# Latent attention with undivided probabilities: each tile's outputs multiplied once by the heads' inverse sums, which are spread over the partitions through memory

## The chip, the core and the metric

The kernel runs on one core of a Trainium2 chip, as one program in one launch. The metric is the device time of that launch in microseconds (us). Before the change three runs took 1687.1, 1684.37 and 1682.98 us; their median, 1684.37 us, is the time before.

A core has a matrix engine (TensorE, in the profile PE, with its weight loads as PEld), a vector engine (VectorE, DVE), a scalar engine (ScalarE, ACT), a general engine (GpSimd, POOL) and a synchronizing engine (SP). Each runs its own instructions in order and waits for the others through semaphores. SBUF is the working memory of 128 partitions, PSUM the banks that PE writes its results to. DMAs move data between SBUF and the chip's memory; they are issued from the queues of SP, ACT and POOL.

## What is computed

Two layers of a diffusion backbone over 512 latent tokens and a prefix of 256 context tokens, 1024 wide, all in float32. Layer 0 mixes tokens by two groups of heads side by side: gated linear attention, and softmax attention with 8 query heads and 2 key and value heads of 64. Their outputs are joined and go through one output projection, then a SwiGLU block. Layer 1 is a gated recurrence and another SwiGLU block. The change is in the softmax attention of layer 0 alone:

```python
def _softmax_attend(q, k, v):
    s = jnp.einsum('bhgqd,bhkd->bhgqk', q, k, preferred_element_type=jnp.float32) * (ATT_HEAD_DIM ** -0.5)
    p = jax.nn.softmax(s, axis=-1).astype(v.dtype)
    return jnp.einsum('bhgqk,bhkd->bhgqd', p, v)
...
    o_blocks = lax.map(lambda qb: _softmax_attend(qb, k_all, va), q_blocks)
...
    o_lat = jnp.concatenate([a_lat, b_lat], axis=-1)
```

Latent queries see all 768 keys, context queries the 256 context keys. `a_lat` is the gated linear attention's half, `b_lat` the softmax attention's; their concatenation is what the output projection multiplies.

## The kernel before

Tokens lie in six tiles of 128: four latent (0 to 3) and two context (4 and 5). `even_mixer` writes layer 0's order out by hand: each piece of work is a generator under a short name ("x" is `att.context`, "y" is `att.latent`, "t" the transposes of the gated linear attention's outputs, "r1" a readout, "M" a group of modulation columns), and `run` steps them in a written sequence. With `pinned` set, PE keeps exactly that program order. DVE, ACT and POOL are ordered by a scheduler that knows the dependences; what it made of them is shown with the change.

`latent` is a pipeline over 32 heads, eight for each latent tile, one pass of its loop (L296) for a head. In pass i:

- `scores` (L178) computes the scores of head i into a two-bank PSUM tile `S` (two buffers). The keys are stored times -1/8, so the scores are negative and L193 on DVE takes a minimum to find the row's maximum. L195 on ACT exponentiates 128x768 scores into `prob` and sums each row into `asm`. L196 on DVE takes the reciprocal of that sum, L198 on DVE multiplies `prob` by it, in place.
- `turned` (L200) transposes the `prob` of head j = i - 3 on PE, six blocks of 128x128: four into a PSUM tile of two alternating ones, two into a single bank `sc`, and copies both pieces to `probT` (L210): 128x512 by ACT, and 128x256 by DVE for every fourth head (j % 4 == 3), by ACT for the other three.
- `values` (L212) multiplies, a pass after every second head was transposed, the `probT` of two heads by the values: 24 matrix instructions into one quarter of the bank `attO` (`self.po[t]`), head 2n in partitions 0 to 63 and head 2n + 1 in 64 to 127. When the fourth pair of a tile is in, `done` (L231) hands the bank to `put` (L732), which casts it on ACT (L734) and subtracts the cast from it on DVE (L735). The two results are a high and a low part that the output projection reads, since PE's fast float32 format keeps fewer bits.

There are two `sc` banks. Tile t's `attO` is bank t % 2, and the narrow transposes of the heads use the other one; after `done`, `other` (L148) gives them the bank just finished, until the next tile starts on its own. So the first narrow transposes after a tile's end write the bank that `put` reads, and have to wait until both its instructions are through. In the loop this is pass 12, 20 and 28: `done` is called in pass 8t + 11.

Behind the last pass come the output projection's matrix instructions (`oproj`; L1558). Its eight units of weights are loaded by SP (L768), cast on ACT (L769) and subtracted on DVE (L770). The buffers `raw` for the loads number three, so the last unit's load waits for an earlier unit's L770. The first pair of tiles it takes are the context tiles, over units 0 to 3 and then over units 4 to 7.

The 32-partition `gcT`, `gt` and `gd` of `gate_rows` (L638) do elsewhere what the change does here: eight or sixteen columns are transposed on PE, copied by DVE (L650) and stored to memory by ACT's queue (L652); L659 reads a row of it back to all partitions.

Of the kernel before, what the change touches and what calls it, by code (L numbers as in the profile page):

```python
# [8 lines left out]
F32 = mybir.dt.float32  # L9
# [4 lines left out]
ALU = mybir.AluOpType  # L14
# [3 lines left out]
P = 128  # L18
# [6 lines left out]
LT = SEQ // P  # L25
# [8 lines left out]
class Split:  # L34


    def __init__(self, pool):
        self.pool, self.tiles = pool, None
# [95 lines left out]
class Attention:  # L134
# [8 lines left out]

    def __init__(self, net, natq, natk, cat):
        self.net, self.nc, self.natq, self.natk, self.cat = net, net.nc, natq, natk, cat
        self.q, self.k, self.po, self.ended = {}, {}, {}, []

    def other(self):  # L148

# [25 lines left out]
            nc.vector.tensor_tensor(q[half[1 - n], 4 * n : 4 * n + 4, :], pv[half[n]], H.bitcast(F32), op=ALU.subtract)  # L175
        self.q[t] = q

    def scores(self, t, heads, p):  # L178

        nc, net = self.nc, self.net  # L180
        s = net.mm_tile("S")
        nk = p.shape[-1]
        w = 1024 // len(heads)
        for x, hd in enumerate(heads):
            at = w * x
            for ks in self.k[int(t >= LT)]:
                m = ks[0].shape[-1]
                for i, k in enumerate(ks):
                    net.mm(s[:, at : at + m], self.q[t][:, hd, :], k[:, hd // 4, :], start=(i == 0), stop=(i == 1))
                at += m  # L190
        sv = s.rearrange("p (x k) -> p x k", k=w)[:, :, :nk]
        mx, sm, r = (net.sm.tile([P, len(heads)], F32, tag=tag, name=tag) for tag in (("amx", "asm", "ars") if len(heads) == 1 else ("ms4", "ss4", "rs4")))
        nc.vector.tensor_reduce(mx, sv, axis=AX.X, op=ALU.min)  # L193
        for x in range(len(heads)):
            nc.scalar.activation(p[:, x, :], sv[:, x, :], AF.Exp, bias=mx[:, x : x + 1], scale=-1.0, accum_out=sm[:, x : x + 1])  # L195
        nc.vector.reciprocal(r, sm)  # L196
        for x in range(len(heads)):
            nc.vector.tensor_scalar(p[:, x, :], p[:, x, :], r[:, x : x + 1], None, op0=ALU.mult)  # L198

# [28 lines left out]
                    tile_position=(0, 64 * a),  # L228
                )

    def done(self, t):  # L231
        self.ended.append(t)
        self.net.put(self.cat, slice(4, 8), slice(t * P, (t + 1) * P), self.po[t].rearrange("p (j i) -> p j i", j=4))

    def context(self):
        wp = self.net.wp
# [23 lines left out]
        yield  # L260
        queries(LT + 1, "wL")
        scores(0)
        yield
        scores(1)
        yield
        turned(0)
        yield
        scores(2)
        values(0)
        yield  # L270
# [14 lines left out]
    def latent(self, ap):  # L285
        kl = [ap.tile([P, 2, SEQ], F32R, name=f"k{x}") for x in "HL"]
        self.k[0] = [kl] + self.k[1]
        q = lambda t: ap.tile([P, 8, P], F32R, tag="qs", bufs=2, name=f"qs{t}")
        self.keys(0, LT, kl)
        yield  # L290
        self.queries(0, q(0))
        yield

        ahead = 3
        ps, pTs, due = {}, {}, []
        for i in range(8 * LT + ahead + 2):  # L296
            t, hd = divmod(i, 8)
            if t < LT:
                ps[i] = ap.tile([P, NT], F32, tag="prob", bufs=4, name="prob")
                self.scores(t, (hd,), ps[i][:, None, :])  # L300
            j = i - ahead
            if 0 <= j < 8 * LT:
                pTs[j] = ap.tile([P, NTT, P], F32, tag="probT", bufs=4, name="probT")
                self.turned(ps.pop(j), pTs[j], (1,) if j % 4 == 3 else (), self.other())
            if due:
                t0, n, xs = due.pop()
                self.values(t0, n, xs)
                if n == 3:
                    self.done(t0)
            if 0 <= j < 8 * LT and j % 2:  # L310
                due.append((j // 8, j // 2 % 4, [pTs.pop(x) for x in (j - 1, j)]))
            if t + 1 < LT and hd == 4:
                self.queries(t + 1, q(t + 1))
            yield


class Net:
# [420 lines left out]
    def post_norm(self, y, x, gv, cuts=1, done=None):  # L738

        nc = self.nc  # L740
        cs = [slice(D // cuts * i, D // cuts * (i + 1)) for i in range(cuts)]
        tmp = self.wp.tile([P, WU], F32, tag="mraw", bufs=2, name="pn")
        ss = self.sm.tile([P, 4 if cuts > 1 else 1], F32, tag="ss4" if cuts > 1 else "ss", name="sq")[:, :cuts]
        for i, c in enumerate(cs):
            self.sumsq(y[:, c], ss=ss[:, i : i + 1])
            nc.vector.tensor_tensor(tmp[:, c], y[:, c], gv[:, c], op=ALU.mult)
        yield
        if cuts > 1:
            s = self.sm.tile([P, 1], F32, tag="ss", name="ss")
            nc.vector.tensor_reduce(s, ss, axis=AX.X, op=ALU.add)  # L750
            ss = s
        rs = self.rstd(ss, D)
        yield
        for c in cs:
            nc.vector.scalar_tensor_tensor(x[:, c], tmp[:, c], rs, x[:, c], op0=ALU.mult, op1=ALU.add)
            if done is not None:
                done(c)
        yield
# [1444 lines left out]
```

## Time and profile before

| What | Value |
|---|---|
| median of three runs | 1684.37 us (1682.98 to 1687.1) |
| the profiled execution | 1683.48 us, its span 1681.5 us |
| TensorE clock granted over the span | 0.999 |
| PE busy, whole span | 1644.6 us (98%) |
| DVE busy, whole span | 1309.8 us (78%) |
| ACT busy, whole span | 917.5 us (55%) |
| POOL busy, whole span | 121.4 us (7%) |
| the latent attention's 32 passes | about 255.6 to 346.5 us |

The span runs from the first instruction's start to the last one's end; the execution's own time is 1.98 us longer. All times of a timeline count from the span's start. In a timeline row stand start, length, engine, line, operation, what it writes and reads, the count of merged instructions, and in brackets the idle time of the engine before it with what ended it. A group's row ends in its busy time and the mean of one in ns, then the idle time before it.

### The profile page before, as it was taken

What the parts mean: (1) busy time and instruction counts of PE and PEld (TensorE: products, weight loads), DVE (VectorE), ACT (ScalarE), POOL (GpSimd) and SP (SyncE); (2) the same over time, 40 slices, a digit from 0 to 9 for tenths busy, and PEclk for the clock granted to TensorE, in tenths of its full rate; (3) what the DMA queues carried; (4) which work ended last, traced back from release to release, by engine and by line L of the source; (5) the groups of instructions that cost most, each with busy time, mean ns of one, the idle gap of its engine ahead of it and who ended that gap; (6) DMA issues with size and microseconds to landing.
All of it is one profiled execution on the core that took longest, in us unless ns stands there. A gap on an engine that the chain in (4) does not pass through costs nothing.

```text
span 1681.5 us, 32537 instructions
## 1 busy us (share of the span) xinstructions
PE 1644.6 (98%) x13407; PEld 1481.0 (88%) x13407; DVE 1309.8 (78%) x2105; ACT 917.5 (55%) x1560; POOL 121.4 (7%) x129
## 2 busy tenths in 40 slices
PE   6999998999999999999999999999999999999998
PEld 5899997888999999998888888888888899999876
DVE  4889768876898988877668548788775599987887
ACT  4745567836543443445447436666664565555654
POOL 1004110001000000003102000000000100000220
PEclk9999999999999999999999999999999999999999
DMA  9651002164243444348725542121124334333793
GB/s 330 192 155 41 2 27 101 51 207 152 84 147 101 144 143 148 117 150 167 142 73 203 190 129 59 51 64 39 52 64 150 125 111 117 113 101 101 183 206 138
DMA packets 184736, 204.79 MB, mean 122 GB/s; under 512 B 7142, under 2 KB 141836, under 8 KB 184588
## 3 DMA queue, kind: packets, MB, share of 16 engines
q1 hardware_dynamic: 173632, 181.82, 34.3%
q0 software_dynamic: 9024, 17.30, 5.9%
q10 hardware_dynamic: 1932, 3.59, 0.7%
q8 instruction: 105, 1.72, 0.4%
q14 instruction: 43, 0.35, 0.1%
HBM read 193.23 MB, written 9.46 MB: 121 GB/s over the span
## 4 chain that ended last, share of the span: by engine, by line
PE 85%; DVE 7%; ACT 3%; DMA 3%; issue 1%; POOL 0%; ACTq 0%; DVEq 0%; POOLq 0%
PE nat L355 13%; PE a L355 12%; PE ff L355 8%; PE E L355 8%; PE x L355 7%; PE oproj L355 6%; PE o L355 4%; PE D L355 4%; PE b L355 4%; PE fq L355 3%; PE gqk L355 2%; PE pearly L355 2%; PE S L355 2%; PE poh L355 1%; PE attO L355 1%
## 5 line engine op out<-in xcount | busy, mean ns | idle before, releaser
L355 PE MATMUL nat<-wH,x 128*128 128x256 f32 (+2 forms) x968 | 225.5, 321 | 3.0 <-ACT x L734 2.6
L355 PEld LDWEIGHTS nat<-wH,x 128*128 128x128 f32 x968 | 162.2, 190 | 19.2 <-ACT x L734 3.7
L824 ACT CAST wH<-raw 128x1024 fp32r<-128x1024 f32 x120 | 125.0, 1050 | 95.5 <-DVE raw L849 31.4
L825 DVE TENSOR_TENSOR wL<-raw,wH 128x1024 fp32r<-128x1024 f32 x120 | 145.6, 1220 | 21.3 <-ACT wH L824 20.9
L355 PE MATMUL nat<-wL,x 128*128 128x256 f32 (+2 forms) x484 | 153.4, 317 | 0.3 <-DVE wL L770 0.3
L770 DVE TENSOR_TENSOR wL<-raw,wH 128x1024 fp32r<-128x1024 f32 (+1 forms) x83 | 98.7, 1198 | 48.0 <-ACT wH L769 47.1
L355 PE MATMUL ff<-x,wH 128*128 128x512 f32 (+1 forms) x512 | 127.7, 340 | 0.0
L769 ACT CAST wH<-raw 128x1024 fp32r<-128x1024 f32 (+1 forms) x83 | 84.9, 1034 | 68.0 <-PE ff L355 19.9
L668 POOL TENSOR_TENSOR rs<-ms,neghalf 128x1 f32<-128x1 f32 (+2 forms) x62 | 63.5, 1029 | 783.0 <-DVE ms L666 782.9
L355 PE MATMUL oproj<-wH,x 128*128 128x512 f32 x320 | 102.1, 396 | 0.4 <-ACT x L1290 0.4
L355 PEld LDWEIGHTS nat<-wL,x 128*128 128x128 f32 x484 | 92.1, 190 | 6.0 <-DVE wL L770 0.7
L597 DVE SCALAR_TENSOR_TENSOR macc<-mraw,scT,macc 128x1024 f32<-128x1024 f32 x70 | 88.1, 1280 | 10.9 <-DMA mraw<-in_mod_w_dram 10.7
L355 PEld LDWEIGHTS ff<-x,wH 128*128 128x128 f32 x512 | 87.2, 190 | 10.1
L355 PE MATMUL x<-wH,two 128*128 128x512 f32 x280 | 90.5, 392 | 0.9 <-DVE y L1798 0.7
L976 ACT COPY qkh<-arr 128x512 f32<-128x512 f32 x112 | 70.2, 643 | 36.3 <-DVE arr L981 32.1
L1723 POOL DMA_DIRECT2D t<-in_ffn_w_down_dram x36 | 41.8, 1228 | 648.1 <-DVE wL L1757 613.5
L355 PE MATMUL ff<-x,wL 128*128 128x256 f32 (+1 forms) x256 | 86.2, 337 | 0.0
L849 DVE TENSOR_TENSOR raw<-raw 128x512 f32<-128x512 f32 x120 | 82.7, 690 | 2.8
L981 DVE TENSOR_TENSOR arr<-arr,f 128x512 f32<-128x512 f32 x112 | 74.2, 687 | 1.9 <-ACT qkh L976 0.3
L355 PE MATMUL E<-x,wH 128*128 128x384 f32 (+1 forms) x320 | 70.9, 311 | 0.0
L355 PEld LDWEIGHTS oproj<-wH,x 128*128 128x128 f32 x320 | 59.5, 188 | 12.6 <-ACT x L1290 0.9
L355 PE MATMUL b<-x,wH 128*128 128x384 f32 (+1 forms) x320 | 70.5, 309 | 0.0
(420 smaller groups left out, 4540.7 us busy)
## 6 DMA issues: line engine op xcount, KB each, us to landing
mraw<-in_mod_w_dram SPq DMA_DIRECT2D x80, 512.0 KB, 4.4
raw<-in_ffn_w_gate_dram SPq DMA_DIRECT2D x44, 512.0 KB, 4.6
raw<-in_ffn_w_up_dram SPq DMA_DIRECT2D x44, 512.0 KB, 4.3
raw<-in_odd_w_in_dram SPq DMA_DIRECT2D x40, 512.0 KB, 3.8
t<-in_ffn_w_down_dram POOLq DMA_DIRECT2D x30, 512.0 KB, 8.0
raw<-in_ffn_w_down_dram SPq DMA_DIRECT2D x28, 512.0 KB, 7.4
mraw<-in_mod_w_dram SPq DMA_DIRECT2D x32, 256.0 KB, 6.3
raw<-in_even_w_in_dram SPq DMA_DIRECT2D x16, 512.0 KB, 3.8
```

The source lines that it names most:

```text
L355: return self.pin(self.nc.tensor.matmul(*a, **k))
L597: nc.vector.scalar_tensor_tensor(a, u, w, a, op0=ALU.mult, op1=ALU.add)
L668: nc.gpsimd.tensor_tensor(rs, ms, self.neghalf.to_broadcast([P, w]), op=ALU.pow)
L769: nc.scalar.copy(H[:, :m], raw[:, :m])
L770: nc.vector.tensor_tensor(L[:, :m], raw[:, :m], H[:, :m].bitcast(F32), op=ALU.subtract)
L824: self.nc.scalar.copy(H, f)
L825: self.nc.vector.tensor_tensor(L, f, H.bitcast(F32), op=ALU.subtract)
L849: add = lambda o, x, y: nc.vector.tensor_tensor(o, x, y, op=ALU.add)
L976: nc.scalar.copy(qkv[:, :, :, half, :], dst)
L981: nc.vector.tensor_tensor(dst, dst, tb, op=ALU.mult)
L1723: add = lambda o, src: self.pin(nc.gpsimd.dma_start(out=o, in_=src, accum_op=ALU.add))
```

## The change

The probabilities stay undivided. `scores` for a latent head writes the reciprocal of the row sum into one column of a tile `rs` of eight columns, one tile of them for each latent tile, and returns; L198 is no longer called there. The columns stand in the order of the output rows: first the four even heads, then the four odd ones. After the last head of a tile, in the next pass, `divisors` transposes the 128x8 reciprocals on PE into a PSUM tile `rT`, copies the 8x128 rows to SBUF on DVE, stores them by POOL's queue to a buffer `rd` in memory, and loads them back by two DMAs of POOL's queue, each of which spreads one row of 512 over 64 partitions of a tile `over`. `done` then multiplies the bank `attO` by `over` on DVE into a tile `att` in SBUF, and `put` casts and subtracts `att` instead of the bank. Besides this, the narrow copy of `probT`, 128x256, is DVE's for all 32 heads. The context's attention is unchanged.

```diff
@@ scores
-    def scores(self, t, heads, p):
+    def scores(self, t, heads, p, given=None):
...
-        nc.vector.reciprocal(r, sm)
+        nc.vector.reciprocal(r if given is None else given, sm)
+        if given is not None:
+            return
         for x in range(len(heads)):
             nc.vector.tensor_scalar(p[:, x, :], p[:, x, :], r[:, x : x + 1], None, op0=ALU.mult)
@@ new, and done
+    def divisors(self, ap, t, r):
+
+        nc, net = self.nc, self.net
+        pt = net.tr_tile("rT")
+        net.tr(pt[:8, :P], r, net.ident)
+        rows = ap.tile([8, P], F32, tag="rT", bufs=2, name="rT")
+        nc.vector.tensor_copy(rows, pt[:8, :P])
+        rd = net.dr.tile([2, 4 * P], F32, name=f"rd{t}")
+        nc.gpsimd.dma_start(out=rd.rearrange("a (n q) -> (a n) q", n=4), in_=rows)
+        self.over[t] = ap.tile([P, 4 * P], F32, tag="over", bufs=2, name="over")
+        for a in range(2):
+            nc.gpsimd.dma_start(out=self.over[t][64 * a : 64 * a + 64], in_=rd[a : a + 1, :].to_broadcast([64, 4 * P]))
+
-    def done(self, t):
+    def done(self, t, ap=None):
         self.ended.append(t)
-        self.net.put(self.cat, slice(4, 8), slice(t * P, (t + 1) * P), self.po[t].rearrange("p (j i) -> p j i", j=4))
+        f = self.po[t]
+        if ap is not None:
+            f = ap.tile([P, 4 * P], F32, tag="att", bufs=1, name="att")
+            self.nc.vector.tensor_tensor(f, self.po[t], self.over[t], op=ALU.mult)
+        self.net.put(self.cat, slice(4, 8), slice(t * P, (t + 1) * P), f.rearrange("p (j i) -> p j i", j=4))
@@ latent, the loop
-                self.scores(t, (hd,), ps[i][:, None, :])
+                if hd == 0:
+                    rs[t] = ap.tile([P, 8], F32, tag="rs", bufs=2, name="rs")
+                x = 4 * (hd % 2) + hd // 2
+                self.scores(t, (hd,), ps[i][:, None, :], rs[t][:, x : x + 1])
...
-                self.turned(ps.pop(j), pTs[j], (1,) if j % 4 == 3 else (), self.other())
+                self.turned(ps.pop(j), pTs[j], (1,), self.other())
...
-                    self.done(t0)
+                    self.done(t0, ap)
...
+            if hd == 0 and 0 < t <= LT:
+                self.divisors(ap, t - 1, rs[t - 1])
```

The new file's lines stand up to 24 lower than before. PE's order at the end of tile 0, from the scores of pass 8 to the values that close the tile in pass 11, before:

```order
L358 MATMUL pT<-ident,prob 128x128 x6
L355 MATMUL S<-kH,qs_3808 128x512
L355 MATMUL S<-kL,qs_3808 128x512
L355 MATMUL S<-kc,qs_3808 128x256 x2
L358 MATMUL pT<-ident,prob 128x128 x6
L355 MATMUL attO<-probT,natk 64x128 x12
L358 MATMUL catT<-ident,gvo 128x128 x4
```

and of the changed kernel:

```order
L382 MATMUL pT<-ident,prob 128x128 x6
L382 MATMUL rT<-ident,rs 8x128
L379 MATMUL S<-kH,qs_3804 128x512
L379 MATMUL S<-kL,qs_3804 128x512
L379 MATMUL S<-kc,qs_3804 128x256 x2
L382 MATMUL pT<-ident,prob 128x128 x6
L379 MATMUL attO<-probT,natk 64x128 x12
L382 MATMUL catT<-ident,gvo 128x128 x4
```

The one transpose `rT` is put in behind the transposes of pass 8; PE's other instructions keep their order here. (`catT` are the transposes of the gated linear attention's outputs, `gvo`.)

DVE's order at the same place, around the values that close tile 0, before (`amx` is the row's extreme score, `x` the parts for the output projection):

```order
L210 COPY probT<-pT 128x256
L193 TENSOR_REDUCE amx<-S 128x1
L196 RECIPROCAL ars<-asm 128x1
L198 TENSOR_SCALAR prob<-prob,ars 128x768
L196 RECIPROCAL ars<-asm 128x1
L198 TENSOR_SCALAR prob<-prob,ars 128x768
L193 TENSOR_REDUCE amx<-S 128x1
L735 TENSOR_TENSOR x_3656<-attO,x_3655 128x4x128
```

and of the changed kernel:

```order
L212 COPY probT<-pT 128x256
L193 TENSOR_REDUCE amx<-S 128x1
L196 RECIPROCAL rs<-asm 128x1
L212 COPY probT<-pT 128x256
L251 TENSOR_TENSOR att<-attO,over 128x512
L196 RECIPROCAL rs<-asm 128x1
L193 TENSOR_REDUCE amx<-S 128x1
L759 TENSOR_TENSOR x_3656<-att,x_3655 128x4x128
```

The two scalings are gone, a second narrow copy has come in, and the multiplication by `over` is the first instruction to read the bank `attO`, ahead of a reciprocal and of the next row extreme. The subtraction behind it reads SBUF.

ACT's order at the end of the stage, from the last copies of `probT` to the casts of the output projection's last four units, before:

```order
L210 COPY probT<-pT 128x512
L734 CAST x_3655<-attO 128x4x128
L659 DMA gv_4860<-gd_1288 128x1024
L659 DMA gv_4862<-gd_1288 128x1024
L1559 ACT_TABLE_LOAD
L769 CAST wH<-raw 128x1024 x4
```

and of the changed kernel:

```order
L212 COPY probT<-pT 128x512 x4
L683 DMA gv_4876<-gd_1288 128x1024
L683 DMA gv_4878<-gd_1288 128x1024
L758 CAST x_3655<-att 128x4x128
L1583 ACT_TABLE_LOAD
L793 CAST wH<-raw 128x1024 x4
```

The two gate loads went ahead of the cast, which now waits for the multiplication on DVE; the table load and the four casts stand behind it as before. On POOL's queue the store `rd` and the two loads `over` of a tile stand together, and those of tiles 1 to 3 behind one readout's power (L668).

More of the change, by code (lines that the diff above doesn't have):

```diff
@@ L145, in __init__ @@
         self.net, self.nc, self.natq, self.natk, self.cat = net, net.nc, natq, natk, cat
-        self.q, self.k, self.po, self.ended = {}, {}, {}, []
+        self.q, self.k, self.po, self.over, self.ended = {}, {}, {}, {}, []
     def other(self):
@@ L294, in latent @@
         ahead = 3
-        ps, pTs, due = {}, {}, []
+        ps, pTs, rs, due = {}, {}, {}, []
         for i in range(8 * LT + ahead + 2):
```

## The prediction

> **What bounds the kernel now.** I read the windows first, over the 32 passes of the latent attention, and beside them the page's chain that ended last, by engine. The columns of a window are its length and, for PE, PEld, DVE, ACT and POOL, busy time and count, then the granted clock, the DMA share and GB/s.
>
> ```profile
> core 0: us, PE busy (x) PEld busy (x) DVE busy (x) ACT busy (x) POOL busy (x), PEclk, DMA share, GB/s
> 255.60:346.50 90.90, 85.60 (x854) 71.08 (x852) 75.34 (x140) 68.73 (x145) 1.28 (x1) 1.00 0.24 82
> PE 85%; DVE 7%; ACT 3%; DMA 3%; issue 1%; POOL 0%; ACTq 0%; DVEq 0%; POOLq 0%
> ```
>
> PE is busy for 85.60 of 90.90 us at full clock. DVE, from which the change takes most, has 15 us to spare. So the stage can only give back what PE waits, some 5.3 us or 0.3% of the kernel. The timeline of PE shows where; these are all its gaps over 0.1 us:
>
> ```profile
> 258.50 0.66 PE L355 MATMUL attO<-probT,natk 128*64 128x128 f32 x8 [1.37 <-DVE probT L210]
> 264.65 0.41 PE L358 MATMUL pT<-ident,prob 128*128 128x128 f32 x2 [0.27 <-DVE x L735]
> 272.13 0.44 PE L358 MATMUL catT<-ident,gvo 128*128 128x128 f32 x2 [0.19 <-ACT probT L210]
> 283.11 0.44 PE L358 MATMUL pT<-ident,prob 128*128 128x128 f32 x2 [0.27 <-DVE probT L210]
> 287.65 0.41 PE L358 MATMUL pT<-ident,prob 128*128 128x128 f32 x2 [1.30 <-DVE x L735]
> 306.22 0.50 PE L355 MATMUL S<-kH,qs 128*128 128x512 f32 x1 [0.42 <-ACT prob L195]
> 311.77 0.66 PE L358 MATMUL qT<-ident,natq 128*128 128x128 f32 x4 [0.51 <-ACT probT L210]
> 331.06 0.44 PE L358 MATMUL pT<-ident,prob 128*128 128x128 f32 x2 [0.50 <-DVE x L735]
> 337.67 0.44 PE L358 MATMUL pT<-ident,prob 128*128 128x128 f32 x2 [0.28 <-DVE probT L210]
> ```
>
> They sum to 5.11 us. The first two belong to the context attention's tail, which the change leaves alone: 3.47 us are in reach. The largest, 1.30 and 0.50, are the narrow transposes of the pass after tiles 0 and 2, held by the subtraction that still reads their bank.
>
> **The work that leaves DVE and ACT.** Groups of the same stretch, and the copy that elsewhere does what `rT`'s will:
>
> ```profile
> L193 DVE TENSOR_REDUCE amx<-S 128x1 f32<-128x768 f32 x32 | 30.4, 951 | 1.6 <-PE S L355 1.5
> L198 DVE TENSOR_SCALAR prob<-prob,ars 128x768 f32<-128x768 f32 x32 | 19.6, 616 | 0.6
> L196 DVE RECIPROCAL ars<-asm 128x1 f32<-128x1 f32 x32 | 5.1, 158 | 5.2 <-ACT prob L195 5.0
> L210 DVE COPY probT<-pT 128x256 f32<-128x256 f32 x8 | 3.3, 412 | 3.2 <-PE pT L358 3.2
> L735 DVE TENSOR_TENSOR x<-attO,x 128x512 fp32r<-128x512 f32 x5 | 3.4, 684 | 0.0
> L195 ACT ACTIVATE prob<-S,amx 128x768 f32<-128x768 f32 x32 | 29.1, 909 | 7.7 <-DVE amx L193 7.6
> L195 ACT ACTIVATION_READ_ACCUMULATOR prob<-S,amx 128x1 f32 x32 | 6.5, 204 | 0.0
> L210 ACT COPY probT<-pT 128x256 f32<-128x256 f32 x24 | 9.2, 383 | 0.5 <-PE pT L358 0.3
> L650 DVE COPY gt<-gcT x4: 272/279/279, 112.4 to 987.9; 16x128 f32<-16x128 f32 x2, 8x128 f32<-8x128 f32 x2
> ```
>
> DVE loses 19.6 us and gains 24 x 0.412 = 9.9, four multiplications of the bank's shape, priced as L735 at 0.68 (2.7), and four copies of 0.28 (1.1): 5.9 less. ACT loses 9.2. Nearly all of it lies under PE and is worth nothing by itself. What it can close are the three gaps that ACT's queue made, 0.19 + 0.42 + 0.51: I take them whole, **-1.1**, bounds 0 and -1.1.
>
> Against it: each narrow copy holds the only narrow bank, and on DVE it stands behind a row extreme of 0.95. Two of the present eight made PE wait (0.27, 0.28). The narrow transposes follow each other quickest after an odd head, 16 of the 32. Bounds: none waits, -0.55; all 16 wait, 16 x 0.28 - 0.55 = +3.9. The present rate gives 8 of 32, 2.2 - 0.55 = +1.65; since a pass on DVE gets shorter (0.62 of scaling out, 0.31 of copying in on average) I take half, **+0.8**.
>
> **The transposes.** The first two rows show pass 8's six transposes and the scores behind them, the others the last values of tile 0 (pass 11), the scores of pass 12 and the subtraction that ends the use of the bank:
>
> ```profile
> 276.13 0.82 PE L358 MATMUL pT<-ident,prob 128*128 128x128 f32 x6
> 276.70 0.48 PE L355 MATMUL S<-kH,qs 128*128 128x512 f32 x1
> 283.48 1.53 PE L355 MATMUL attO<-probT,natk 128*64 128x128 f32 x24
> 284.94 0.50 PE L355 MATMUL S<-kH,qs 128*128 128x512 f32 x1
> 286.82 0.68 DVE L735 TENSOR_TENSOR x<-attO,x 128x512 fp32r<-128x512 f32 x1
> ```
>
> Six take 0.57 us of PE, so four `rT` cost 4 x 0.1 = **+0.4**. Nothing hides them, as PE is the bound.
>
> **The bank.** Today it comes free when ACT's cast and DVE's subtraction are done, at 287.50, 2.56 us after the last values (284.94). PE wanted it at 287.65 - 1.30 = 286.35, 1.4 after. Afterwards one multiplication frees it, about 0.1 + 0.68 = 0.8 us after the values, if `over` is there. Then both gaps close: **-1.8**. That depends on the round trip through memory, which has no like in this trace. The time it has, from `rT` on PE to the last values, at tiles 0, 1 and 2 (276.70 to 284.94 above, then these):
>
> ```profile
> 300.87 0.38 PE L358 MATMUL modT<-ident,modrows 128*128 128x128 f32 x2
> 309.24 0.66 PE L358 MATMUL catT<-ident,gvo 128*128 128x128 f32 x4
> 321.22 0.60 PE L358 MATMUL catT<-ident,gvo 128*128 128x128 f32 x4
> 329.15 0.50 PE L355 MATMUL S<-kH,qs 128*128 128x512 f32 x1
> ```
>
> That is 8.2, 8.4 and 7.9 us. At tiles 0 and 2 `rT`'s copy stands behind one narrow copy, so transpose, both copies and semaphores take 1.0 off; at tile 1 it stands behind the reciprocal of pass 16, which needs that pass's extreme (0.95) and exponential (0.91 and 0.20), 2.0 off. Left are 7.2, 6.4 and 6.9. The chain is one store, then, when that has landed, two loads issued one after the other. Nearest rows: small loads on ACT's queue (L405, 0.5 to 48 KB; the first row), and POOL's (L1723), which are 256 or 512 KB and add into their target:
>
> ```profile
> DMA to landing us min/median/max: 1.6/2.9/4.3
> L1723 POOL DMA_DIRECT2D t<-in_ffn_w_down_dram x36: 909/1206/2057, 765.6 to 1628.2; - x36
> DMA to landing us min/median/max: 4.0/8.0/16.3
> ```
>
> Lower end 1.6 + 0.9 + 1.6 = 4.1 us, upper end with POOL's fastest 4.0 + 0.9 + 4.0 = 8.9. I take the small loads' median, as 4 and 128 KB are nearer to them: 2.9 + 0.9 + 2.9 = 6.7. `over` is then 0.3 late at tile 1 alone, under the 0.6 us that the bank has in hand (1.4 - 0.8).
>
> The Trainium skill ("DMA: Bandwidth & Descriptors", section on the anatomy of a DMA on the gpsimd path) gives a fixed cost of about 2.0 us for each such DMA plus bytes over 436 GB/s. By it an estimate of the trip is 2.0 + 0.9 + 2.3 = 5.2, and the sum below would be 0.5 better. The same section warns that the receipt of a write to memory can take surprisingly long, which is the first rival's side. No run here shows either for such transfers yet.
>
> **The stage's end.** Tile 3's trip has less time, and ACT's cast of `att` stands ahead of the table load and four casts of output weights:
>
> ```profile
> 339.91 0.47 PE L355 MATMUL oproj<-wH,x 128*128 128x512 f32 x1
> 346.51 13.60 PE oproj L355 x59
> 346.55 0.59 ACT L734 CAST x<-attO 128x512 fp32r<-128x512 f32 x1 [1.83 <-PE attO L355]
> 348.69 2.95 ACT L769 CAST wH<-raw 128x1024 fp32r<-128x1024 f32 x3
> 351.03 0.33 SPq L768 DMA_DIRECT2D raw<-in_even_w_out_dram  x1
> 354.66 1.05 ACT L769 CAST wH<-raw 128x1024 fp32r<-128x1024 f32 x1 [3.01 <-DMA raw<-in_even_w_out_dram]
> 355.74 1.23 DVE L770 TENSOR_TENSOR wL<-raw,wH 128x1024 fp32r<-128x1024 f32 x1 [2.47 <-ACT wH L769]
> ```
>
> `rT` goes in about 340.2, its row is copied by 341.2, and the values end at 346.5: 5.3 us. A trip of 6.7 is 1.4 late, and with 0.8 for the multiplication the cast moves by 2.2. Behind it move the casts, the load at 351.03 that waits for a buffer of theirs, and the last unit, ready today at 356.97. PE runs 48 instructions over units 0 to 3 (four of them ahead of 346.51, the first at 339.91) and nine over units 4 to 6 before it needs that unit: 346.51 + 53 x 0.2305 = 358.7. Slack 1.7, so PE waits **+0.5**; bounds 0 (trip under 6.2) and 8.9 - 5.3 + 0.8 - 1.7 = 2.7.
>
> **Sum:** -1.1 + 0.8 + 0.4 - 1.8 + 0.5 = -1.2 us in the profiled execution's 1683.48. The median of the runs, 1684.37, stands 0.9 above that, so I predict **1683.2 us**. Behind the stage the output projection is PE's without a gap, so a gain stays.
>
> **Rivals.**
> - *The round trip is long* and `over` becomes the wait. DVE is in order: behind the blocked multiplication stand a reciprocal, the next row extreme and so the scores' banks; PE stops at the narrow transposes. With r for the trip, PE waits r - 7.8, r - 7.4 and r - 7.5 after tiles 0 to 2 (the times left, plus the bank's 0.6; 0.4 more at tile 1 for `catT`) and r - 6.2 at the end. Break-even is about r = 7.6; at the slowest small load's 4.3 us, r = 9.5: 1.7 + 2.1 + 2.0 + 3.3 - 1.7 = +7.4, **1691.8 us**. For it: three DMAs in a row, two of them waiting for one. Against it: the queue and the DMA engines are nearly empty here (share 0.24).
> - *The narrow bank becomes the bound*: all 16 copies hold PE, 3.9 in place of 0.8, **1686.3 us**. Against it: PE needs 8.24 / 3 = 2.7 us for a pass at 276.70, DVE some 0.95 + 0.16 + 0.41 = 1.5.
> - *Everything closes*: the 3.47 us of gaps less 0.4, **1681.3 us**. For it: ACT and DVE both have less in every pass. Against it: every multiplication must find `over` landed.
> - *It does not do what it says*: the columns, `rd` and `over` are each written once per tile before use, so I see no second pass that would keep the scaling.
>
> **How the numbers follow.** Forecast 0.50, long trip 0.25, narrow bank 0.11, all closed 0.12, others 0.02. A measurement of this kernel can tell about 0.3%, 5.05 us, from no change: bounds 1679.3 and 1689.4. No case but "others" reaches the first, since PE's gaps are too small: faster 0.05. Slower needs r above 8.9, most of the first rival and a little of the second: 0.25. Within 0.3%: 0.70. The range goes from 1680.5, just under the fastest case, to 1690.5, which takes in POOL's 8.9 and part of the rival.
>
> **What would show it.** In the changed profile L198 has no latent rows; DVE's busy time in the stage is near 69.5 and ACT's near 59.5; PE's gaps after tiles 0 and 2 are gone; `over`'s second load lands about 6.7 us after `rT`'s copy. If the multiplication's idle time is put down to `over`'s DMA after every tile, the first rival holds. If PE's narrow transposes wait for L212 in most odd passes, the second does. A gain above 3.5 us would mean that PE's busy time itself shrank, which no step here has.

## The result and the profile after

The changed kernel takes 1689.97 us (median of 7 runs, 1688.89 to 1690.51), the kernel before 1684.37 (7 runs, 1682.98 to 1687.1): 1.0033 of it, 95% interval 1.0024 to 1.0042, or 5.6 us slower. The prediction was 1683.2. The first rows of the profile after:

```profile
span 1688.2 us, 32581 instructions
PE 1645.6 (97%) x13411; PEld 1481.1 (88%) x13411; DVE 1303.7 (77%) x2105; ACT 911.7 (54%) x1536; POOL 127.9 (8%) x141
```

DVE and ACT have each lost 6 us over the span (1309.8 and 917.5 before), PE is as busy as it was (1644.6), and the span is 6.7 us longer. So it is waiting of PE that was added. Lines of the changed kernel from L198 on stand 2 to 24 lower than before: L210 is L212, L355 is L379, L358 is L382, L769 is L793. New are the sums' row (L239), its store (L241), the two loads (L244) and the multiplication (L251).

Windows say where; the columns are those of the prediction's first fence. After, the latent passes and then the output projection with what is beside it:

```profile
256.00:347.00 91.00, 85.60 (x844) 71.08 (x846) 69.24 (x140) 63.73 (x122) 7.21 (x12) 1.00 0.28 91
347.00:425.00 78.00, 73.11 (x350) 57.51 (x347) 47.06 (x57) 34.50 (x68) 10.41 (x12) 1.00 0.51 166
```

Before, for the second:

```profile
345.50:420.00 74.50, 74.50 (x366) 61.10 (x363) 49.91 (x61) 37.41 (x72) 9.66 (x11) 1.00 0.56 180
```

In the passes PE is idle for 5.4 us of 91 (91.00 - 85.60), where the window of the prediction has 5.3: nothing gained, nothing lost. In the output projection, where PE had no gap at all, it now waits 78.00 - 73.11 = 4.9 us. Who ends PE's waits between 250 and 430 us of the changed kernel (sum, count, longest; four rows are left out, three that the kernel before has too and one of 0.2 for `qT`, which waits for DVE):

```profile
PE oproj L379 <- ACT wH L793: 2.1, 2, 1.7
PE pT L382 <- DVE rT L239: 1.4, 1, 1.4
PE hT L382 <- DVE xn L719: 1.3, 1, 1.3
PE oproj L379 <- DVE wL L794: 1.1, 3, 0.8
PE pT L382 <- DVE probT L212: 0.7, 3, 0.3
PE oproj L379 <- DVE ms L690: 0.5, 1, 0.5
PE catT L382 <- ACT probT L212: 0.4, 1, 0.4
PE modT L382 <- ACT probT L212: 0.4, 1, 0.4
PE pT L382 <- DVE att L251: 0.3, 1, 0.3
```

The four rows of `oproj` and `hT` sum to 5.0 and are the 4.9 us. Of them 3.2 are for the weights of units 4 to 7 (`wH`, `wL`), the largest, 1.7, for the last unit; the 1.8 of `ms` and `xn` come behind the context tiles' outputs. The row of 1.4 for `rT` is a wait in the loop that the prediction doesn't have. How the last tile ends, from the timelines of the engines and queues:

```profile
342.26 0.33 SPq L792 DMA_DIRECT2D raw<-in_even_w_out_dram  x1
342.68 0.86 SPq L1536 DMA_DIRECT2D xr<-in_ctx_dram  x2
342.72 0.28 DVE L239 COPY rT<-rT 8x128 f32<-8x128 f32 x1
343.29 0.53 POOL L241 DMA_DIRECT2D rd<-rT  x1 [16.15 <-DVE rT L239]
348.36 0.82 ACTq L683 DMA_DIRECT2D gv<-gd  x2
349.36 1.06 POOL L244 DMA_DIRECT2D over<-rd  x2 [5.54 <-DMA rd<-rT]
355.17 0.69 DVE L251 TENSOR_TENSOR att<-attO,over 128x512 f32<-128x512 f32 x1 [8.63 <-DMA over<-rd]
355.89 0.62 ACT L758 CAST x<-att 128x512 fp32r<-128x512 f32 x1 [9.36 <-DVE att L251]
357.82 2.94 ACT L793 CAST wH<-raw 128x1024 fp32r<-128x1024 f32 x3
360.16 0.33 SPq L792 DMA_DIRECT2D raw<-in_even_w_out_dram  x1
363.81 1.04 ACT L793 CAST wH<-raw 128x1024 fp32r<-128x1024 f32 x1 [3.04 <-DMA raw<-in_even_w_out_dram]
```

The sums' row is out of PSUM at 343.0, `over` is there at 355.1: a trip of 12.1 us, for the predicted 6.7. ACT stands for 9.4 us before the cast, and behind it are the weight casts (348.69 before, 357.82 now), the load that needs their buffer (351.03, now 360.16) and the last unit (354.66, now 363.81). The time from issue to landing, of the store and then of the two loads, for tile 2, then the two loads for tile 1, then both for tile 3:

```profile
DMA to landing us min/median/max: 1.5/1.5/1.5
DMA to landing us min/median/max: 2.7/2.8/2.8
DMA to landing us min/median/max: 3.8/4.6/5.3
DMA to landing us min/median/max: 5.8/5.8/5.8
DMA to landing us min/median/max: 5.2/5.3/5.4
```

The same 4 KB and 128 KB, on the same queue. At tile 3 the store was issued at 343.29, up to 1.0 us behind three loads of 512 KB on SP (342.26 to 343.54), and the two loads 1 us behind two more of 512 KB on ACT's queue. At tile 1 weight loads on SP ran beside the two loads. The share of the DMA engines in the changed kernel goes with it: 0.14 and 0.10 around the trips of tiles 0 and 2 (278 to 285 and 323 to 330 us), 0.38 at tile 1 (303 to 311) and 0.62 at tile 3 (342 to 349).

The kernel before had the same loads at this place, and nearly the same share, as three rows of its SP and ACT queues and a window show:

```profile
339.64 0.33 SPq L768 DMA_DIRECT2D raw<-in_even_w_out_dram  x1
340.06 0.86 SPq L1512 DMA_DIRECT2D xr<-in_ctx_dram  x2
346.55 0.82 ACTq L659 DMA_DIRECT2D gv<-gd  x2
339.00:346.00 7.00, 6.97 (x78) 5.36 (x74) 2.32 (x6) 3.91 (x9) 0.00 (x0) 1.00 0.64 225
```

The wait in the loop is at tile 1; timelines of POOL, DVE and PE:

```profile
300.11 0.27 PE L382 MATMUL rT<-ident,rs 128*8 128x128 f32 x1
300.27 1.03 POOL L692 TENSOR_TENSOR rs<-ms,neghalf 128x4 f32<-128x4 f32 x1 [18.15 <-DVE ms L690]
301.34 0.69 DVE L1217 TENSOR_TENSOR gvo<-gvo,rs 128x512 f32<-128x512 f32 x1 [0.35 <-POOL rs L692]
302.28 0.68 DVE L1219 SCALAR_TENSOR_TENSOR gvo<-gvo,og 128x512 f32<-128x512 f32 x1
302.88 0.15 DVE L196 RECIPROCAL rs<-asm 128x1 f32<-128x1 f32 x1
302.95 0.26 DVE L239 COPY rT<-rT 8x128 f32<-8x128 f32 x1
303.27 0.88 PE L382 MATMUL pT<-ident,prob 128*128 128x128 f32 x6 [1.37 <-DVE rT L239]
```

`rT` is written into one of the two banks that alternate for PE's transposes. Its copy on DVE came behind the readout of the gated tile, which waits for POOL, and ended at 303.21, 3.1 us after PE began `rT`. PE's next `pT` stood until that bank was free.

### The profile page after: what moved, and what is told of

Same layout as the page of the kernel before. It is cut to its first block, busy times and chain, and to the rows that moved or that the text cites. A ratio compares the mean times of both kernels' runs of the same rounds, so it can differ in the third digit from the quotient of the medians.

```text
span 1688.2 us, 32581 instructions
## 1 busy us (share of the span) xinstructions
PE 1645.6 (97%) x13411; PEld 1481.1 (88%) x13411; DVE 1303.7 (77%) x2105; ACT 911.7 (54%) x1536; POOL 127.9 (8%) x141
## 4 chain that ended last, share of the span: by engine, by line
PE 82%; DVE 7%; DMA 4%; ACT 3%; issue 3%; POOL 1%; DVEq 0%; ACTq 0%; POOLq 0%
PE nat L379 13%; PE a L379 11%; PE ff L379 8%; PE E L379 8%; PE x L379 7%; PE o L379 4%; PE b L379 4%; PE D L379 4%; PE oproj L379 4%; PE fq L379 3%; PE gqk L379 2%; PE pearly L379 2%; PE q L379 2%; PE S L379 1%; PE poh L379 1%
## 5 line engine op out<-in xcount | busy, mean ns | idle before, releaser
L379 PE MATMUL nat<-wH,x 128*128 128x256 f32 (+2 forms) x968 | 226.8, 323 | 3.0 <-ACT x L758 2.6
L379 PEld LDWEIGHTS nat<-wH,x 128*128 128x128 f32 x968 | 163.3, 191 | 19.3 <-ACT x L758 3.7
L379 PE MATMUL nat<-wL,x 128*128 128x256 f32 (+2 forms) x484 | 154.0, 318 | 0.3 <-DVE wL L794 0.3
L379 PE MATMUL ff<-x,wH 128*128 128x512 f32 (+1 forms) x512 | 127.7, 340 | 0.0
L793 ACT CAST wH<-raw 128x1024 fp32r<-128x1024 f32 (+1 forms) x83 | 84.9, 1035 | 68.4 <-PE ff L379 19.9
L379 PE MATMUL oproj<-wH,x 128*128 128x512 f32 x320 | 103.1, 397 | 2.9 <-ACT wH L793 2.1
L379 PEld LDWEIGHTS nat<-wL,x 128*128 128x128 f32 x484 | 92.8, 192 | 6.0 <-DVE wL L794 0.7
L379 PEld LDWEIGHTS ff<-x,wH 128*128 128x128 f32 x512 | 87.3, 190 | 10.0
L379 PE MATMUL x<-wH,two 128*128 128x512 f32 x280 | 90.5, 392 | 0.8 <-DVE y L1822 0.7
L1000 ACT COPY qkh<-arr 128x512 f32<-128x512 f32 x112 | 70.1, 642 | 36.4 <-DVE arr L1005 32.2
L379 PE MATMUL ff<-x,wL 128*128 128x256 f32 (+1 forms) x256 | 86.2, 337 | 0.0
L379 PEld LDWEIGHTS oproj<-wH,x 128*128 128x128 f32 x320 | 59.4, 188 | 16.2 <-ACT wH L793 2.9
L379 PE MATMUL E<-x,wH 128*128 128x384 f32 (+1 forms) x320 | 70.9, 311 | 0.0
L379 PE MATMUL b<-x,wH 128*128 128x384 f32 (+1 forms) x320 | 70.6, 309 | 0.0
```

The lines of the kernel that those rows point to most:

```text
L379: return self.pin(self.nc.tensor.matmul(*a, **k))
L793: nc.scalar.copy(H[:, :m], raw[:, :m])
L1000: nc.scalar.copy(qkv[:, :, :, half, :], dst)
```

## The experiments

Each profiled execution is cut at three places, so that stretches compare without what lies ahead of them: the start of POOL's last copy of the keys ("kL", L164), the start of the last matmul of the latent outputs (`attO`), that of the last matmul of the output projection (`oproj`), and the end of the span. The kernel before stands first. Times and ratios are those of the timed rounds; each ratio is to the kernel before in the same round, whose median was 1683.80 to 1684.37 us.

| kernel | median us | ratio to before, 95% interval | kL to attO | attO to oproj | oproj to end |
|---|---|---|---|---|---|
| before | 1684.37 | | 91.8 | 70.1 | 1265.2 |
| changed | 1689.97 | 1.0033 (1.0024 to 1.0042) | 92.1 | 76.8 | 1263.4 |
| e1, last tile divides as before | 1685.05 | 1.0009 (1.0000 to 1.0018) | 93.2 | 70.0 | 1264.9 |
| e2, last tile without load | 1683.49 | 0.9997 (0.9988 to 1.0006) | 91.4 | 70.1 | 1264.5 |
| e3, sums' row on ACT | 1688.03 | 1.0029 (1.0021 to 1.0038) | 90.5 | 76.8 | 1263.8 |
| e4, no division | 1681.57 | 0.9989 (0.9980 to 0.9998) | 89.4 | 70.6 | 1264.8 |
| e5, last put later | 1683.35 | 0.9999 (0.9990 to 1.0008) | 92.7 | 70.1 | 1264.1 |
| e6, large loads later | 1690.41 | 1.0047 (1.0034 to 1.0059) | 92.1 | 76.3 | 1263.9 |
| e7, narrow copies as before | 1691.76 | 1.0049 (1.0036 to 1.0062) | 91.7 | 76.6 | 1266.0 |
| e8, e5 and e3 together | 1681.95 | 0.9993 (0.9984 to 1.0002) | 90.5 | 70.0 | 1266.2 |
| e9, changed again | 1689.85 | 1.0032 (1.0019 to 1.0045) | 91.8 | 77.3 | 1263.7 |
| e10, e8 with e7's copies | 1685.01 | 1.0001 (0.9992 to 1.0010) | 92.2 | 69.9 | 1265.7 |
| e11, e8 again | 1681.97 | 0.9989 (0.9980 to 0.9998) | 90.5 | 70.0 | 1266.6 |

From the start to kL every kernel here runs the same instructions in the same order (e2 one memset more), yet the executions differ there by up to 2.1 us (254.42 before, 255.92 changed, 256.53 in e5). So 1.5 of the 6.7 us between the two spans are no effect of the change; from kL on it is 1432.3 - 1427.1 = 5.2 us, near the timed 5.6. The last column moves by 3 us between kernels whose code there is the same. It is at its shortest, 1263.4 to 1263.9, in four of the kernels whose projection ends late, but e7 has 1266.0; why is not shown.

The projection's stretch grew by 6.7 us (70.1 to 76.8), more than the 4.9 us that PE is idle there, with the same matmuls in it. An estimate from the rows accounts for it: a matmul of the projection that starts after a wait is on record for 0.50 us, while undisturbed ones start 0.23 us apart, so each of the seven waits costs about 0.25 us beyond what counts as idle.

### e1: the last tile divides as before

```diff
-                self.scores(t, (hd,), ps[i][:, None, :], rs[t][:, x : x + 1])
+                self.scores(t, (hd,), ps[i][:, None, :], rs[t][:, x : x + 1] if t < LT - 1 else None)
...
-                    self.done(t0, ap)
+                    self.done(t0, ap if t0 < LT - 1 else None)
...
-            if hd == 0 and 0 < t <= LT:
+            if hd == 0 and 0 < t < LT:
```

> Tiles 0 to 2 as changed; tile 3 (the last) divides its probabilities row by row as the kernel before does, so that it has no round trip through memory. Theory A (the last tile's trip took 12 us for the 6.7 of the prediction, its cast came 9 us late on ScalarE, and the output projection lost about 4.9 us in PE waits that the kernel before doesn't have): the waits of the output projection are gone, 1684.5 to 1685.5 us, 4.5 to 5.5 below the changed kernel's 1690.0. Rival B (the loss lies in the loop, in the 32 narrow copies on VectorE and the transposition of the sums): no more than 1 us below the changed kernel, 1689 to 1690. Rival C (half and half): about 1687.

It took 1685.05, and the projection is back at 70.0 us. Its window shows PE without a gap:

```profile
347.00:425.00 78.00, 78.00 (x387) 64.32 (x388) 52.19 (x64) 37.74 (x74) 10.74 (x11) 1.00 0.57 191
```

The last tile carries nearly all of the loss; rivals B and C fall. The loop is 1.1 us longer than the changed kernel's (93.2 for 92.1), and PE's waits for DVE's narrow copies are 1.7 us for 0.7, so the last tile's eight scalings are not free on DVE beside these copies.

### e2: the last tile without its load

```diff
+        self.over[LT - 1] = ap.tile([P, 4 * P], F32, tag="over1", bufs=1, name="over1")
+        nc.gpsimd.memset(self.over[LT - 1], 1.0)
...
         nc.gpsimd.dma_start(out=rd.rearrange("a (n q) -> (a n) q", n=4), in_=rows)
+        if t == LT - 1:
+            return
```

> All as changed, but tile 3's outputs are multiplied by a tile of ones that was set before the loop, in place of the inverse sums read back from memory (left out: tile 3's division; its store is still made). The multiplication and the cast no longer wait for a transfer. Theory A: the transfer's lateness is the whole loss at the stage's end, 1684.5 to 1686 us. Rival D (the multiplication on VectorE between the last output and the cast, and POOL's issues, cost something without the transfer): 1687 to 1689. Rival B: 1689 to 1690.

1683.49 us, 1.0 under the expected range, and 70.1 for the projection. Multiplication, cast and store are as in the changed kernel, so it is the loaded sums that cost, not the work at the end. Rivals B and D fall. Whether it is the wait for them or their traffic this run can't tell, since both are gone; e5 can.

### e3: the sums' row copied by ScalarE

```diff
-        nc.vector.tensor_copy(rows, pt[:8, :P])
+        nc.scalar.copy(rows, pt[:8, :P])
```

> All as changed, but the copy of the turned sums out of PSUM is on ScalarE, not on VectorE, where it stood behind operations that wait for POOL at tile 1 and held one of the two alternating banks. Theory A: PE's wait of 1.4 us for that bank at tile 1 is gone, so 1688.4 to 1689.2 us; the stage's end stays as late (about 5 us). Rival E (that wait is covered again by the next one, which VectorE ends anyway): no change, 1689.6 to 1690.4.

1688.03 us, 0.4 under theory A's range. The wait of 1.4 us for `rT` is gone from the list of PE's waits, the 0.3 for `att` with it, and the loop is 1.6 us shorter (90.5 for 92.1; the changed kernel's second profile has 91.8). The timed difference, 1.0029 for 1.0033, lies inside the intervals. The gain is shown by the traces, not by these times; rival E falls by them, and the projection stays at 76.8.

### e4: no division

```diff
-            if hd == 0 and 0 < t <= LT:
-                self.divisors(ap, t - 1, rs[t - 1])
...
-                    self.done(t0, ap)
+                    self.done(t0)
```

> No latent tile is divided at all: neither the probabilities nor the outputs (left out: the division of the four latent tiles, with the turned sums, the store, the loads and the multiplications). The narrow copies stay on VectorE. This is what undivided probabilities are worth if the division cost nothing. Theory A: below the kernel before by the closed gaps less the narrow copies, 1682 to 1684 us. Rival B (narrow copies cost the loss): 1687 or above.

1681.57 us, 0.9989 of before, 0.4 under the expected range; rival B falls. That is what undivided probabilities give in this arrangement when their division costs nothing: about 1.9 us.

### e5: the last tile's put behind the weight casts

The last tile's inverse sums lie in a work buffer, multiplied in place; the call that multiplies and casts moves from the last pass to the output projection, behind the casts of its eight units.

```diff
+        if t == LT - 1:
+            self.over[t] = net.wp.tile([P, WU], F32, tag="mraw", bufs=2, name="over3")[:, : 4 * P]
...
+                elif n == 3:
+                    self.net.last = lambda: self.done(LT - 1, ap)
...
+            units.append(self.rows_unit(w, c) if c < 4 else self.rows_unit(w, c, wop))
+            if c == 7 and self.last is not None:
+                with self.tc.issue_after(self.cast[0].ins), self.tc.issue_after(self.cast[1].ins):
+                    self.last()
```

> All as changed (the last tile too goes through memory), but its multiplication and its cast stand behind the casts of the output projection's last four weight units on ScalarE and VectorE, not ahead of them; its inverse sums lie in another buffer so that this order is free. Theory A (the trip's 12 us cost time only because ScalarE and VectorE, which work in order, hold the weight casts behind it): the trip stays as long, PE's waits of 4.9 us at the start of the output projection are gone, 1683.5 to 1685.5 us (kernel before 1683.8 in the last runs, changed kernel 1.0033 of it). Rival F (the transfers' own traffic, with the weights' load and the context's rows late because of it, is the cost): 1687 to 1690.

1683.35 us, 0.15 under the expected range. Timelines of POOL's queue and ACT, then the window of the projection:

```profile
344.45 0.53 POOL L241 DMA_DIRECT2D rd<-rT  x1 [16.15 <-DVE rT L239]
350.97 1.06 POOL L247 DMA_DIRECT2D over<-rd  x2 [5.99 <-DMA xr<-in_ctx_dram]
351.65 2.95 ACT L799 CAST wH<-raw 128x1024 fp32r<-128x1024 f32 x3
358.10 1.05 ACT L799 CAST wH<-raw 128x1024 fp32r<-128x1024 f32 x1 [3.50 <-DMA raw<-in_even_w_out_dram]
361.05 0.63 ACT L764 CAST x<-over 128x512 fp32r<-128x512 f32 x1 [1.89 <-DVE over L254]
```

```profile
347.00:425.00 78.00, 78.00 (x388) 64.02 (x386) 52.32 (x64) 38.08 (x73) 11.82 (x13) 1.00 0.60 194
```

The store was issued 6.5 us ahead of the loads, so the trip is as long as it was; but the weight casts no longer stand behind it, and PE has no gap in the projection. The cast of the last tile comes at 361.05, 5 us later than in the changed kernel, and costs nothing: the projection takes the context tiles and tiles 0 and 1 first. The lateness is harmful only through the order of ACT and DVE. Rival F falls.

### e6: the large loads later

```diff
         xt = pp.tile([P, D], F32, tag="xt", bufs=2 if nxt and isinstance(nxt[2], Forms) else 4, name=f"xr{t}")
+        if hold is not None and t >= LT:
+            nc.vector.tensor_copy(xt[:, :1], hold[1][:, 0, :1].bitcast(F32))
...
+        if hold is not None:
+            self.nc.scalar.copy(gv[:, :1], hold[0][:, 0, :1].bitcast(F32))
```

where `hold` is the last tile's place in `cat`, so that the loads into `xt` and `gv` wait for its cast.

> All as changed, but the four 512 KB loads that are issued while the last tile's trip is under way (two of the context's rows on SP, two of the gate's rows on ScalarE's queue) wait for the last tile's cast; one 512 KB weight load stays ahead of the store. Theory A (the store of 4 KB lands after 5.8 us, not 1.5 to 1.8, and the two loads after 5.3, not 2.8, because the large loads were issued just ahead of them): store 1.5 to 4 us, loads 2.7 to 3.4, att begins 4 to 7 us earlier against the turned sums' copy, and most of the 4.9 us of waits goes: 1684.5 to 1687 us. Rival G (the lateness is of POOL's own path at this place, whatever is loaded beside it): landings stay at 5 to 6 us and the time at 1689 to 1690.

The landings of tile 3's store and loads, and then ACT and SP:

```profile
DMA to landing us min/median/max: 4.2/4.2/4.2
DMA to landing us min/median/max: 2.7/2.7/2.8
```

```profile
351.95 0.62 ACT L760 CAST x<-att 128x512 fp32r<-128x512 f32 x1 [5.31 <-DVE att L251]
353.56 0.81 SPq L1540 DMA_DIRECT2D xr<-in_ctx_dram  x2
354.97 2.95 ACT L795 CAST wH<-raw 128x1024 fp32r<-128x1024 f32 x3
357.31 0.33 SPq L794 DMA_DIRECT2D raw<-in_even_w_out_dram  x1
362.60 1.04 ACT L795 CAST wH<-raw 128x1024 fp32r<-128x1024 f32 x1 [4.67 <-DMA raw<-in_even_w_out_dram]
```

The landings are as theory A has them: without the four loads `over` lands in 2.7 us, as at tile 2, and the store, with one load ahead, in 4.2 for 5.8 (0.2 above the expected range); the cast is some 4 us earlier than in the changed kernel. G falls by the landings. The time that theory A expected did not come: 1690.41 us. The held loads now lie ahead of the last weight load (5.3 us from its issue to the cast that waits for it, 3.65 in the changed kernel), so that this cast is only 1.2 us earlier, and PE waits 3.9 us in the projection for 4.9: 1.5 for the weights (3.2 in the changed kernel) and 2.4 behind the context tiles (1.8). The 1.0 that was left isn't in the time. In this profile it is hidden by the granted clock, which a window shows at half for 3.4 us of the projection:

```profile
365.90:369.30 3.40, 3.40 (x10) 2.64 (x9) 2.72 (x3) 0.00 (x0) 0.00 (x0) 0.50 0.86 267
```

By an estimate, half of 3.4, that costs 1.7 us. The changed kernel's first profile has no such stretch; its second, e9, has one as long, and against it e6's projection is 1.0 us shorter (76.3 for 77.3). The mean clocks of e6's timed executions, 0.996 to 0.998 where the changed kernel's are 0.997 to 0.999, hint at more such stretches, but don't say where they lie. Moving the contention did not remove the loss.

### e7, e10: the narrow copies as before

```diff
-                self.turned(ps.pop(j), pTs[j], (1,), self.other())
+                self.turned(ps.pop(j), pTs[j], (1,) if j % 4 == 3 else (), self.other())
```

> All as changed, but of the 32 narrow copies out of the single bank three in four are on ScalarE again, as in the kernel before. Theory A (the prediction's term of +0.8 us for the narrow copies on VectorE, bounds -0.55 to +3.9): 0.5 to 1.5 us below the changed kernel, about 1688.5 to 1689.2. Rival H (freed VectorE makes their move free or a gain): equal to the changed kernel or up to 3 us above it.

The loop is 0.4 us shorter than in the changed kernel's first profile (0.1 than in its second): `rT`'s wait of 1.4 is gone (fewer copies stand ahead of its copy on DVE), and four waits for ACT's copies, 1.1 us in all, take its place. The timed runs are 1.8 us above the changed kernel's, with intervals that overlap, and theory A's range is missed; in the profile the longer time lies behind the projection (1266.0 for 1263.4 and 1263.7), where the code is the same. So a second pair compares the copies without `rT`'s wait:

> The last tile's put behind the weight casts and the turned sums' copy on ScalarE, and three in four of the narrow copies on ScalarE as in the kernel before. Theory A (narrow copies on VectorE cost 0.4 to 0.8 us): the loop about 90.0 us for the 90.5 of the same kernel with all of them on VectorE, and the time 0.4 to 0.8 us below it. Rival H (their move is a gain, as the two timed runs hint: 1691.8 for 1690.0): the loop no shorter, 0.5 to 2.5 us above it. Rival I (within what can be told): both within 0.4 us.

Here the loop is 92.2 us for 90.5 and the time 1685.01 for 1681.97 on the same chip (1.0001 for 0.9989, intervals that still touch). The largest row of e10's waits of PE that e11 doesn't have:

```profile
PE pT L388 <- ACT probT L212: 1.2, 4, 0.6
```

So with the sums' row off DVE, the narrow copies on DVE are a gain of 1.7 us in the loop (e8 and e11 have 90.5 both, e10 is one profile); rival H holds there. With the sums' row on DVE, in the changed kernel, they cost 0.1 to 0.4, below theory A's 0.5 to 1.5.

### e8, e11: put later and row on ScalarE

> The last tile's put behind the weight casts (as in the run before) and the copy of the turned sums on ScalarE (as in the run that did this alone, which gave 0.7 us). Theory A: the two add up, 1682.5 to 1684.5 us, at or below the kernel before, with the kernel that divides nothing (1681.6) as the floor. Rival: one hides the other, no better than the put alone.

> The same as the run with the last put behind the weight casts and the turned sums' copy on ScalarE, again: is it below the kernel before by more than the runs scatter? Theory A: ratio 0.9990 to 0.9998 to the kernel before, about 7 us below the changed kernel; rival: the 0.9993 was chance, 1.0000 to 1.0010.

The two edits add: 90.5 us of loop, as in e3, and 70.0 of projection, as in e5. The first time, 1681.95, is 0.55 under the expected range, the second ratio 0.0001 under its own. Two measurements give 0.9993 and 0.9989, that is 1.2 and 1.9 us below the kernel before; the second interval ends under 1, the first just above it. The second is e4's ratio, so little more is to be had from this change; in the profiles e4's loop and projection together are still 0.5 us shorter (160.0 for 160.5). The changed kernel beside e11 stood at 1689.85 (the run e9):

> The changed kernel once more, beside the two that follow, so that they can be told apart on one chip. Theory A: 1689 to 1691 us, 1.0033 of the kernel before; kL's last cast to the last output matmul of the latent tiles about 92.1 us, from there to the last matmul of the output projection about 76.8.

## Why the prediction was wrong

The kernel was forecast 1.2 us faster and came 5.6 us slower. The time lies inside the stated range, whose upper end took in trips of 8.9 us at every tile. That it does is luck: the trip was long at one tile only, and there it was longer than that.

- **The stage's end, +0.5.** This is the step that failed. It took 6.7 us for tile 3's trip, from small loads' median, and "1.4 late". The trip was 12.1 us, PE waited 4.9 us in the projection, and the stretch grew by 6.7. The chain that it names (the cast, the table load, the weight casts, the load behind them, the last unit) is the one that came late; its cost was ten times too small. By the prediction's own rule for this place, r - 6.2, PE would wait 5.9 for the last unit. The rule counts that unit as ready with its low part (L770), while PE waited for the high part (`wH`), 1.2 us sooner, which leaves 4.7. The trace has 3.2 us of idle time up to that unit, in five waits, and their restarts by the estimate above another 1.2. The 1.8 behind the context tiles (`ms`, `xn`) are not in the prediction; e1, e2 and e5 don't have them either, so they come with the late end. These three runs each remove the lateness in another way, and each brings the projection back to 70.
- **Why the trip was mis-sized.** Against the long trip the prediction had set the DMA share of 0.24. That is a mean over 91 us; from 339 to 346 us, just before the values end, it was 0.64. At this one place SP issues 1.5 MB within 1.3 us and ACT 1 MB more. The prediction quotes the row at 351.03, but not the loads at 339.64, 340.06 and 346.55. At tiles 0 and 2, without such neighbours, the trip was near what it was taken to be: 1.8 and 1.5 for the store, 2.7 to 3.0 for the loads, 6.2 and 5.7 in all. The Trainium skill ("DMA: Bandwidth & Descriptors", section on issuing engines that are not separate DMA queues) says that transfers of all issuers share the same 16 engines and interleave; the landings at tile 3 and in e6 agree. The Trainium skill's fixed cost of about 2.0 us per transfer (same page, section on the anatomy of a DMA on the gpsimd path), from which the prediction worked out 5.2 for the trip, is near the landings at tile 2 (1.5 and 2.8) and not those at tile 3 (5.8 and 5.3).
- **The bank, -1.8.** Right: PE's waits of 1.30 and 0.50 after tiles 0 and 2 are gone. At tile 1 `att` held PE for 0.3: the sums' copy ended 3.1 us after `rT`, where 2.0 was counted, and the loads took up to 5.3. The prediction had foreseen tile 1 as the tight one.
- **The transposes, +0.4.** Too narrowly seen. It counted PE's 0.1 us each and not the bank that each takes until its copy is made: 1.4 us at tile 1. The prediction had placed that copy behind pass 16's reciprocal (the "2.0 off"), but used it for the trip only. e3 removes it, and the 0.3 of `att` with it: 1.6 us of loop.
- **ACT's three gaps, -1.1.** Not closed: in their place stand two others of 0.4 that end with ACT's copies (the rows `catT` and `modT`). ACT's busy time in the stage is 63.7, where 59.5 was forecast: 24 copies of 383 ns sum to 9.2, but operations of ACT that follow each other overlap in the records (six copies from 339.75 on in the kernel before, three wide and three narrow, take 2.73 us for the 2.9 of their means), and busy time counts an overlap once: the window lost 5.0. DVE's 69.2 is near the forecast 69.5.
- **Narrow copies, +0.8.** PE's waits for DVE's narrow copies went from 0.6 to 0.7 us only, so what it was counted from did not come. In the changed kernel the copies cost 0.1 to 0.4 (e7), by the wait for `rT` that their place on DVE brings, less the waits for ACT that they save. Without that wait the sign turns: a gain of 1.7 (e10 against e11).
- **The loop's sum.** -1.7 was forecast without the last tile, +0.3 came (92.1 for 91.8). The terms as read: -1.8 for the bank, +0.4 for the transposes on PE, +1.4 for `rT`'s bank, +0.3 for tile 1's `att`, -0.3 for ACT's gaps, +0.2 for narrow copies, +0.2 for `qT`'s wait for DVE: +0.4.
- **Rivals.** The long trip, with 1691.8 us, was right for the last of its four waits and wrong for the other three: the trip did not grow everywhere, and PE's waits after tiles 0 to 2 were 0, 0.3 and 0. The narrow bank did not become the bound. "Everything closes" (3.1 us below the kernel before) was not reached; e8 and e11, with the two edits that the changed kernel lacks, come to 1.2 and 1.9 us below it.

## What to carry to other kernels

A small transfer's landing time is read from what is issued just ahead of it on every queue, in the timeline of the place where it will run, and not from a mean share or a median over the kernel. Where such a transfer ends in front of in-order work that does not need it, put its consumer behind that work: in e5 the last tile's cast came 5 us later still and PE did not wait. A tile that is added to a rotating pool of banks costs not only its matmul, but the wait of the next user until its copy is through the queue it stands in.

## What the runs showed of the hardware

- A 4 KB store issued by POOL landed after 1.5 to 1.8 us at tiles 0 and 2 in every profile that has it, after 1.7 to 2.9 at tile 1 (one 512 KB load issued 1.2 to 3.5 us ahead of it), after 4.2 with one 512 KB load issued 1.0 us ahead of it, and after 5.2 to 6.1 with three. The 128 KB loads that follow landed after 2.7 to 3.1 at tiles 0 and 2 and in e6, and after 4.4 to 5.7 at tile 3 beside 512 KB loads.
- POOL's issue of such a store takes 0.53 to 0.76 us and of one of the two loads some 0.53, where the larger ones of L1723 took 0.91 or more.
- The granted clock fell to half for 3.4 us at a time: once in the first 30 us of some executions (25.4 to 28.8 us in the changed kernel's first profile; the mean over these 30 us is 0.94 there and in e4, e5 and e10), and once within the output projection in two others (0.50 over 365.9 to 369.3 us in e6, 0.51 over 363.5 to 367.0 in e9). In e9 PE was waiting for the last weight unit when it began (1.5 us), in e6 such waits (1.0 and 0.5) had ended 0.9 us before; but the changed kernel's first profile waited 1.7 there at full clock. What brings it is not shown.
